# Score products with the keys' low parts: from zero-padded operands on 128 rows of the array to 64 rows, one row half for each half of the keys

## The chip, the core and the metric

The kernel runs on one core of a Trainium2 chip. The metric is the time of one execution on the device in microseconds, as the median of several runs. The engines are named as in the profile: PE is the tensor engine (its matmuls), PEld its weight loads, DVE the vector engine, ACT the scalar engine, POOL GpSimd, and SP the engine that issues most of the DMAs.

## The reference

One layer over 1024 positions of width 1024. The input is normalised and modulated, projected, mixed by 16 attention heads of width 64 in two groups, gated, projected back, added to the input and normalised again. Eight heads (FoX) use a softmax with a forget bias, eight (stick-breaking) a product of sigmoids:

```python
def _fox_block(q, k, v, f_q, f_k, q_pos, k_pos):
    s = jnp.einsum('bhqd,bhkd->bhqk', q, k).astype(jnp.float32) * scale
    s = s + (f_q[..., :, None] - f_k[..., None, :])
    p = jax.nn.softmax(jnp.where(causal, s, -jnp.inf), axis=-1)
    return jnp.einsum('bhqk,bhkd->bhqd', p.astype(v.dtype), v)

def _stick_breaking_block(q, k, v, q_pos, k_pos):
    z = jnp.einsum('bhqd,bhkd->bhqk', q, k).astype(jnp.float32) * scale
    log_keep = jnp.where(strict, jax.nn.log_sigmoid(-z), 0.0)
    later = lax.cumsum(log_keep, axis=3, reverse=True) - log_keep
    w = jnp.where(strict, jnp.exp(jax.nn.log_sigmoid(z) + later), 0.0)
    return jnp.einsum('bhqk,bhkd->bhqd', w.astype(v.dtype), v)

h = u @ w_in[layer]                # queries, keys, values, gates of both groups
# per block of 128 queries: the two functions above, over the keys up to the block's end
y = concat(y_fox * silu(fg), y_sb * silu(sg)) @ w_out[layer]
x = layer_norm(alpha * x + gate * y)
```

Both groups begin with the scores q times k over a head's 64 components. These score products are what the change is about.

## The kernel before

All operands are float32. To keep precision at the fast rate, the kernel splits an operand into a high part, rounded to the type float32r, and a low part, the rest, and forms three of the four products: high x high, low x high and high x low. The projections do so with three matmuls per step (L255 to L257).

For the scores, the head's 64 components fill only half of the array's 128 rows, so two of the three products share one matmul. For each pair of heads p and each head h in it, the query tile `qst[p][h]` holds the scaled queries' high part on the head's own 64 partitions (`r` in the code) and their low part on the other 64 (`o`); the key tile `kst[p][h]` holds the keys' high part on both halves (ScalarE writes one, a DMA copies it to the other, L240 to L242). One matmul over 128 rows (L410) thus gives high x high plus low x high.

The third product, the queries' high part times the keys' low part, is a second matmul into the same place (L411). The keys' low parts of both heads of a pair lie in one tile, `klo[p]`: head 0 on partitions 0 to 63, head 1 on 64 to 127 (L243). As stationary operand it takes a tile `z` of 128 partitions out of `qz`: the head's own 64 partitions hold the block's queries, copied by ScalarE for every block (`att_query`, L388), and the other 64 hold zeros, set once at the start by GpSimd (L100 to L102), so that the other head's low parts count for nothing.

The work is cut into units (p, h, i): 8 pairs, 2 heads, 8 blocks of 128 queries, 128 units in all. Unit i needs the keys up to `ke = (i + 1) * 128`. Its scores go to the tile `S`, two PSUM banks of 512 columns, of which there is one for the whole kernel. Up to 512 keys fill one bank; more are cut into two equal parts, one in each bank (`ns`, `w`). Pairs 0 to 3 are stick-breaking heads: ScalarE reads `S` twice (L430, L431). Pairs 4 to 7 are FoX heads: VectorE reads it once (L417). Later, lagging two units, PE transposes the weights (L461) and multiplies them with the values (`att_pv`, L476); there the low parts' products use 64 columns of the array.

The order on PE is written out by hand: in a loop over the units, each unit's score products are followed by a measured number of steps of the remaining matmul work (projections of later pairs, the output projection, called fillers), the transposes of an earlier unit, and value products. The query copy of the next unit is issued right behind a unit's scores. The other engines' order is set by a scheduler that also places the waits.

Of the kernel before, what the change touches and what calls it, by code (L numbers as in the profile page):

```python
# [8 lines left out]
F32 = mybir.dt.float32  # L9
F32R = mybir.dt.float32r  # L10
AF = mybir.ActivationFunctionType
ALU = mybir.AluOpType

P = 128
# [4 lines left out]
HD = 64  # L19
# [8 lines left out]
def tile_hybrid_layer(  # L28
# [17 lines left out]
    nc = tc.nc  # L46
# [9 lines left out]
    def att_tile(name, dt=F32):  # L56
        return big("att", 6, name, dt)
# [13 lines left out]
    def s_tile(name):  # L71
        return ps.tile([P, 2, 512], F32, tag="S", bufs=1, name=name)
# [8 lines left out]
    def after(*instructions):  # L81
        stack = ExitStack()
        for i in instructions:
            stack.enter_context(tc.issue_after(i.ins))
        return stack
# [11 lines left out]
    nc.gpsimd.memset(half.bitcast(F32), 0.5)  # L97

    qz = [[cp.tile([P, P], F32R, tag=f"qz{h}{b}", name=f"qz{h}{b}") for b in range(2)] for h in range(2)]
    for h in range(2):  # L100
        for t in qz[h]:
            nc.gpsimd.memset(t.bitcast(F32), 0.0)  # L102
    gate = cp.tile([P, D], F32, tag="gate", name="gate")
    mhalf = cp.tile([P, 1], F32, tag="mhalf", name="mhalf")
    nc.gpsimd.memset(mhalf, -0.5)
# [55 lines left out]
    for kt in range(NB):  # L161
        nc.tensor.matmul(sc_all[:, kt // 4, kt % 4 * P:][:, :P], sc[:, kt:kt + 1].to_broadcast([P, P]), ident,
                         start=True, stop=True)
# [71 lines left out]
    def evac_k(p, ch, acc, kst, klo, heads):  # L235
        s = slice(ch * 512, ch * 512 + 512)
        for h in heads:
            r = slice(h * HD, h * HD + HD)
            o = slice((1 - h) * HD, (1 - h) * HD + HD)
            first = nc.scalar.copy(kst[h][r, s], acc[r, :])  # L240
            kf = kst[h].bitcast(F32)
            nc.sync.dma_start(kf[o, s], kf[r, s])  # L242
            last = nc.vector.tensor_tensor(klo[r, s], acc[r, :], kf[r, s], op=ALU.subtract)  # L243
        return first, last

    def evac_g(p, ch, acc, sg):
# [12 lines left out]
    qst, kst, klo, sgt, vt = {}, {}, {}, {}, {}  # L259
# [11 lines left out]
    def evac_m(p, m, ch, acc, heads=(0, 1)):  # L271
        if m == 0:
            evac_q(p, ch, acc, qst[p], heads)
        elif m == 1:
            return evac_k(p, ch, acc, kst[p], klo[p], heads)
        else:
            evac_g(p, ch, acc, sgt[p])
# [102 lines left out]
    zq = {}  # L380
    turn = [0, 0]

    def att_query(u):
        p, h, i = u
        zq[u] = z = qz[h][turn[h] % 2]
        turn[h] += 1
        r = slice(h * HD, h * HD + HD)
        nc.scalar.copy(z[r, :], qst[p][h].bitcast(F32)[r, i * P:i * P + P])  # L388

    def att_causal(u):  # L390
        p, h, i = u
        if p >= 4:
            f = fb[2 * (p - 4) + h]
            dg = slice(i * P, i * P + P)
            nc.vector.tensor_tensor(f[:, dg], f[:, dg], ps_causal[0][:, :P] if ps_causal else causal, op=ALU.add)

    def att_scores(u, following):
        p, h, i = u
        z = zq.pop(u)
        ke = (i + 1) * P  # L400
        ns = 1 if ke <= 512 else 2
        w = ke // ns
        qs = slice(i * P, i * P + P)
        dg = slice(ke - P, ke)
        if p >= 4:
            f = fb[2 * (p - 4) + h]
        S = s_tile(f"S_{p}_{h}_{i}")
        for s in range(ns):
            ks = slice(s * w, s * w + w)
            nc.tensor.matmul(S[:, s, :w], qst[p][h][:, qs], kst[p][h][:, ks], start=True, stop=False)  # L410
            nc.tensor.matmul(S[:, s, :w], z, klo[p][:, ks], start=False, stop=True)  # L411
        v3 = lambda a: a[:, :ke].rearrange("p (a b) -> p a b", a=ns)
        if p >= 4:
            a = att_tile(f"a_{p}_{h}_{i}")
            nm = sb.tile([P, 1], F32, tag="nm", bufs=4, name=f"nm_{p}_{h}_{i}")
            l = sb.tile([P, 1], F32, tag="l", bufs=4, name=f"l_{p}_{h}_{i}")
            rows = nc.vector.tensor_tensor_reduce(out=v3(a), in0=S[:, :ns, :w], in1=v3(f),  # L417
                                           op0=ALU.add, op1=ALU.min, scale=-1.0, scalar=BIG,
                                           accum_out=nm)
            if following:  # L420
                with after(rows):
                    att_causal(following)
            nc.scalar.activation(a[:, :ke], a[:, :ke], AF.Exp, scale=-1.0, bias=nm, accum_out=l)  # L423
            nc.vector.reciprocal(l, l)  # L424
            nc.gpsimd.tensor_scalar(a[:, :ke], a[:, :ke], l, 1.0, op0=ALU.mult, op1=ALU.mult)  # L425
            st_w[u] = a
        else:
            kp = att_tile(f"kp_{p}_{h}_{i}")
            be = att_tile(f"be_{p}_{h}_{i}")
            nc.scalar.activation(v3(kp), S[:, :ns, :w], AF.Sigmoid, scale=-1.0)  # L430
            nc.scalar.activation(v3(be), S[:, :ns, :w], AF.Sigmoid)  # L431


            n = min(ke, 512)
            rv = kp[:, ke - n:ke][:, ::-1]
            scan = nc.vector.tensor_tensor_scan(rv, rv, floor[0][:, 512 - n:][:, ::-1], initial=0.0,  # L436
                                                op0=ALU.mult, op1=ALU.max)
            if ke > n:
                rv = kp[:, :ke - n][:, ::-1]
                scan = nc.vector.tensor_tensor_scan(rv, rv, floor[0][:, 0:1].to_broadcast([P, ke - n]),  # L440
                                                    initial=kp[:, ke - n:ke - n + 1], op0=ALU.mult, op1=ALU.max)
            with after(scan):
                att_causal(following)
            nc.gpsimd.tensor_tensor(be[:, :ke - 1], be[:, :ke - 1], kp[:, 1:ke], op=ALU.mult)  # L444
            nc.gpsimd.memset(be[:, ke - 1:ke], 0.0)
            st_w[u] = be
# [195 lines left out]
    for kb in range(NB):  # L642
        last = kb == NB - 1
# [95 lines left out]
    for kb in range(NB):  # L739
# [13 lines left out]
        if kb < len(evacs):  # L753
            n, h = evacs[kb]
# [196 lines left out]
    for k in range(len(units) + LAG + 1):  # L951
        if k < len(units):
            if k == 16 * 4 - 1:
                load_fb(0)
                load_fb(1)
            if k == 0:
                att_query(units[0])
            with after(*last_evac if k == 0 else ()):
                att_scores(units[k], units[k + 1] if k + 1 < len(units) else None)
            if k == 16 * 4 - 1:  # L960
                ps_causal.append(ps.tile([P, 512], F32, tag="fl", bufs=1, name="ps_causal"))
                nc.scalar.copy(ps_causal[0][:, :P], causal)
            if k + 1 < len(units):
                att_query(units[k + 1])
            p, h, i = units[k]
            if 4 <= p < NPAIR - 1 and i == 0:
                load_fb(2 * (p - 4) + h + 2)
# [3 lines left out]
        if LAG <= k < len(units) + LAG:  # L971
            u = units[k - LAG]
# [78 lines left out]
```

## Time and profile before

| | |
|---|---|
| median of 3 runs | 691.55 us (691.04 to 691.66) |
| the profiled execution | 691.02 us, of which its span 689.3 us |
| granted clock of PE, mean | 0.996 |
| score products L410, L411 | 192 matmuls each |
| copies of queries into `qz`, L388 | 128 |

A row of the timeline gives start and duration in microseconds, the engine, the line, the operation, what is written from what, and the shape. Of a matmul, `128*128` is the number of array rows times array columns that it uses, and `128x384` the size of the output. Matmuls are pipelined, so that their recorded durations overlap: the distance from one start to the next tells what a matmul takes from the engine. In a row of grouped instructions, the number behind the bar is the busy time in microseconds, then the mean in nanoseconds, then the idle time in front of these instructions.

### The profile page before, as it was taken

To read this page: it belongs to the slowest core of one execution; us is meant where nothing else is said; L and a number is where in the kernel's file an instruction comes from. 1 tells how busy PE (TensorE), PEld (TensorE's weight loads), DVE (VectorE), ACT (ScalarE), POOL (GpSimd) and SP (SyncE) were. 2 spreads that over 40 slices of the span, in tenths; PEclk is the share of its full clock that TensorE was granted. 3 is DMA by queue.
4 is the path that set the end of the run, shared out by engine and by line. 5 is a ranking of instruction groups with operands and counts; after the bars stand their busy time and mean duration, and the time that the engine had idled before them with its cause. 6 is when DMAs were issued, how large, how long until landed. Compare 5 with 4: busy or idle time off the path is not lost. (4 is left out here: it accounts for less than half of the span.)

```text
span 689.3 us, 11785 instructions
## 1 busy us (share of the span) xinstructions
PE 673.6 (98%) x4033; PEld 589.7 (86%) x4033; DVE 453.9 (66%) x923; ACT 379.8 (55%) x858; POOL 430.4 (62%) x556
## 2 busy tenths in 40 slices
PE   8999999999999999999999999999999999999995
PEld 5789898888998888889998888899988889888884
DVE  5985458767656676676675665665566667774644
ACT  5666457856567666575665564655565667521000
POOL 4567977656438565556398897867584364655422
PEclk9999999999999999999999999999999999999998
DMA  8956241011102122112134555353251298153301
GB/s 314 416 225 241 72 121 45 25 40 53 39 9 70 41 55 55 38 49 60 38 137 139 185 166 160 101 165 127 100 150 39 80 310 320 58 175 104 120 31 61
DMA packets 44028, 81.59 MB, mean 118 GB/s; under 512 B 5120, under 2 KB 18880, under 8 KB 43072
## 3 DMA queue, kind: packets, MB, share of 16 engines
q1 hardware_dynamic: 42816, 76.65, 33.8%
q10 hardware_dynamic: 1152, 4.19, 2.0%
q8 instruction: 32, 0.52, 0.3%
q14 instruction: 28, 0.23, 0.1%
HBM read 60.34 MB, written 16.29 MB: 111 GB/s over the span
## 5 line engine op out<-in xcount | busy, mean ns | idle before, releaser
L255 PE MATMUL m<-uh,whi 128*128 128x512 f32 x304 | 126.3, 416 | 0.5 <-DVE kl L243 0.5
L256 PE MATMUL m<-ul,whi 128*128 128x512 f32 x304 | 119.8, 394 | 0.0
L257 PE MATMUL m<-uh,wlo 128*128 128x512 f32 x304 | 119.6, 394 | 0.0
L464 DVE TENSOR_TENSOR pt<-T,pt 128x512 fp32r<-128x512 f32 (+2 forms) x192 | 100.5, 550 | 17.9 <-ACT pt L463 16.8
L444 POOL TENSOR_TENSOR be<-be,kp 128x127 f32<-128x127 f32 (+3 forms) x64 | 77.1, 1205 | 34.5 <-DVE kp L440 24.7
L463 ACT CAST pt<-T 128x512 fp32r<-128x512 f32 (+2 forms) x192 | 85.7, 480 | 16.8 <-PE T L461 13.0
L436 DVE TENSOR_TENSOR_SCAN kp<-kp,floor 128x512 f32<-128x512 f32 (+2 forms) x64 | 65.2, 1018 | 32.1 <-ACT kp L430 31.3
L476 PEld LDWEIGHTS pv<-pt,v 128*128 128x128 f32 (+1 forms) x640 | 77.2, 163 | 4.5 <-DVE pt L464 0.7
L476 PE MATMUL pv<-pt,v 128*128 128x256 f32 (+3 forms) x640 | 80.5, 271 | 0.5 <-DVE pt L464 0.5
L425 POOL TENSOR_SCALAR a<-a,l 128x1024 f32<-128x1024 f32 (+3 forms) x64 | 47.9, 748 | 43.3 <-DVE l L424 29.8
L257 PEld LDWEIGHTS m<-uh,wlo 128*128 128x128 f32 x304 | 57.1, 188 | 13.5
L423 ACT ACTIVATE a<-a,nm 128x1024 f32<-128x1024 f32 (+3 forms) x64 | 49.8, 778 | 34.1 <-DVE nm L417 33.0
L410 PE MATMUL S<-k,q 128*128 128x512 f32 (+5 forms) x192 | 66.5, 348 | 0.2 <-DVE nm L417 0.2
L411 PE MATMUL S<-kl,qz 128*128 128x512 f32 (+5 forms) x192 | 65.5, 342 | 0.0
L255 PEld LDWEIGHTS m<-uh,whi 128*128 128x128 f32 x304 | 57.3, 188 | 9.2 <-DVE kl L243 0.9
L256 PEld LDWEIGHTS m<-ul,whi 128*128 128x128 f32 x304 | 57.4, 189 | 7.9
L497 POOL TENSOR_TENSOR ty<-ty,sg 64x256 f32<-64x256 f32 x64 | 47.4, 741 | 25.4 <-DVE ty L496 12.8
L417 DVE CUSTOM_DVE_ANT_0 a<-S,fb 128x1024 f32<-128x1024 f32 (+3 forms) x64 | 48.3, 755 | 20.4 <-PE S L411 9.3
L430 ACT ACTIVATE kp<-S 128x128 f32<-128x128 f32 (+3 forms) x64 | 41.7, 651 | 31.8 <-PE S L411 28.3
L310 PE MATMUL v<-whi_v,uh 128*128 128x256 f32 (+1 forms) x192 | 56.0, 292 | 0.7 <-DVE kl L243 0.7
L388 ACT CAST qz<-q 64x128 fp32r<-64x128 f32 x128 | 37.4, 295 | 33.0 <-PE S L411 31.9
L312 PE MATMUL v<-wlo_v,uh 128*128 128x256 f32 (+1 forms) x192 | 54.2, 282 | 0.0
(287 smaller groups left out, 1612.9 us busy)
## 6 DMA issues: line engine op xcount, KB each, us to landing
raw<-in_w_qkg_dram SPq DMA_DIRECT2D x38, 256.0 KB, 2.9
wss<-in_w_ss_dram SPq DMA_DIRECT2D x7, 1024.0 KB, 9.1
x<-in_x_dram SPq DMA_DIRECT2D x8, 512.0 KB, 7.0
k<-k SPq DMA_DIRECT2D x32, 128.0 KB, 2.4
wg<-in_w_gate_dram SPq DMA_DIRECT2D x8, 512.0 KB, 4.4
raw_o<-in_w_out_dram SPq DMA_DIRECT2D x16, 256.0 KB, 2.7
fb<-f_dr ACTq DMA_DIRECT2D x8, 512.0 KB, 4.2
wo_dr<-whi_o SPq DMA_DIRECT2D x16, 256.0 KB, 2.4
```

Of the source, the lines that this page charges most:

```text
L255: nc.tensor.matmul(acc, hi[:, c], u_hi[kt][:, s], start=(kt == 0), stop=False)
L256: nc.tensor.matmul(acc, hi[:, c], u_lo[kt][:, s], start=False, stop=False)
L257: nc.tensor.matmul(acc, lo[:, c], u_hi[kt][:, s], start=False, stop=(kt == NB - 1))
L310: nc.tensor.matmul(acc[:, :n], u_hi[kt][:, ts_], hi[:, s], start=(kt == 0), stop=False)
L312: nc.tensor.matmul(acc[:, :n], u_hi[kt][:, ts_], lo[:, s], start=False, stop=(kt == NB - 1))
L410: nc.tensor.matmul(S[:, s, :w], qst[p][h][:, qs], kst[p][h][:, ks], start=True, stop=False)
L411: nc.tensor.matmul(S[:, s, :w], z, klo[p][:, ks], start=False, stop=True)
L436: scan = nc.vector.tensor_tensor_scan(rv, rv, floor[0][:, 512 - n:][:, ::-1], initial=0.0, op0=ALU.mult, op1=ALU.max)
L444: nc.gpsimd.tensor_tensor(be[:, :ke - 1], be[:, :ke - 1], kp[:, 1:ke], op=ALU.mult)
L463: nc.scalar.copy(hi[:, :n, qo:qo + P], t3)
L464: nc.vector.tensor_tensor(lo[:, :n, qo:qo + P], t3, hi.bitcast(F32)[:, :n, qo:qo + P], op=ALU.subtract)
L476: nc.tensor.matmul(acc[:m, q0:256], vt[p][:, kb, h * P:h * P + m], pt[:, kb % 4, q0:], start=start, stop=stop)
```

## The change

The third product now uses 64 rows of the array, without the zeros. For the first 512 keys, the keys' low parts lie on the head's own partitions as before, and the stationary operand is `qst` itself, its 64 partitions with the high part. For the keys from 512 on, the low parts are written to the other 64 partitions (`evac_k`, where `ch` is the half of the keys), and the stationary operand is the tile `z`, into which ScalarE copies the queries on those other partitions. That copy is made only for units with i of 4 or more. The two heads of a pair still share the tile `klo[p]`: where one head has its first half, the other has its second.

A unit with more than 512 keys is now cut at 512: the first bank holds 512 columns, the second the rest. The order of its four products is: high parts for the second bank, high parts for the first bank, low parts for the first bank, low parts for the second bank. The two low products of such a unit use different rows of the array and different banks. The zeroing of `qz` is gone. The readers of `S` take it as one row of `ke` columns.

```diff
     qz = [[cp.tile([P, P], F32R, tag=f"qz{h}{b}", name=f"qz{h}{b}") for b in range(2)] for h in range(2)]
-    for h in range(2):
-        for t in qz[h]:
-            nc.gpsimd.memset(t.bitcast(F32), 0.0)
...
-            last = nc.vector.tensor_tensor(klo[r, s], acc[r, :], kf[r, s], op=ALU.subtract)
+            last = nc.vector.tensor_tensor(klo[o if ch else r, s], acc[r, :], kf[r, s], op=ALU.subtract)
...
     def att_query(u):
         p, h, i = u
+        if i < 4:
+            return
         zq[u] = z = qz[h][turn[h] % 2]
         turn[h] += 1
         r = slice(h * HD, h * HD + HD)
-        nc.scalar.copy(z[r, :], qst[p][h].bitcast(F32)[r, i * P:i * P + P])
+        o = slice((1 - h) * HD, (1 - h) * HD + HD)
+        nc.scalar.copy(z[o, :], qst[p][h].bitcast(F32)[r, i * P:i * P + P])
...
-        ns = 1 if ke <= 512 else 2
-        w = ke // ns
...
-        for s in range(ns):
-            ks = slice(s * w, s * w + w)
-            nc.tensor.matmul(S[:, s, :w], qst[p][h][:, qs], kst[p][h][:, ks], start=True, stop=False)
-            nc.tensor.matmul(S[:, s, :w], z, klo[p][:, ks], start=False, stop=True)
-        v3 = lambda a: a[:, :ke].rearrange("p (a b) -> p a b", a=ns)
+        r = slice(h * HD, h * HD + HD)
+        o = slice((1 - h) * HD, (1 - h) * HD + HD)
+        banks = [(0, min(ke, 512))] + ([(512, ke)] if ke > 512 else [])
+        for b, (k0, k1) in reversed(list(enumerate(banks))):
+            nc.tensor.matmul(S[:, b, :k1 - k0], qst[p][h][:, qs], kst[p][h][:, k0:k1], start=True, stop=False)
+        for b, (k0, k1) in enumerate(banks):
+            w, rows = (zq.pop(u), o) if b else (qst[p][h][:, qs], r)
+            nc.tensor.matmul(S[:, b, :k1 - k0], w[rows, :], klo[p][rows, k0:k1], start=False, stop=True)
+        S = S.rearrange("p a b -> p (a b)")[:, :ke]
...
-            nc.scalar.activation(v3(kp), S[:, :ns, :w], AF.Sigmoid, scale=-1.0)
-            nc.scalar.activation(v3(be), S[:, :ns, :w], AF.Sigmoid)
+            nc.scalar.activation(kp[:, :ke], S, AF.Sigmoid, scale=-1.0)
+            nc.scalar.activation(be[:, :ke], S, AF.Sigmoid)
```

How the order on PE changes is seen at a unit with 768 keys, head 1, block i = 5 of the first pair. In the names, `S` is the score tile, `k`, `q` and `kl` are the tiles `kst`, `qst` and `klo`; the last column is the size of the output. Before:

```order
L461 MATMUL T_1_2_0_1466<-ident,be_1_2_1368 128x128 x3
L410 MATMUL S_1_5_1472<-k_1_249,q_1_247 128x384
L411 MATMUL S_1_5_1472<-kl_250,qz_83 128x384
L410 MATMUL S_1_5_1472<-k_1_249,q_1_247 128x384
L411 MATMUL S_1_5_1472<-kl_250,qz_83 128x384
L255 MATMUL m_2_1_1427<-uh_116,whi_2_1_1243 128x512
```

And after the change:

```order
L463 MATMUL T_1_2_0_1454<-ident,be_1_2_1357 128x128 x3
L408 MATMUL S_1_5_1460<-k_1_245,q_1_243 128x256
L408 MATMUL S_1_5_1460<-k_1_245,q_1_243 128x512
L413 MATMUL S_1_5_1460<-kl_246,q_1_243 128x512
L413 MATMUL S_1_5_1460<-kl_246,qz_83 128x256
L252 MATMUL m_2_1_1415<-uh_112,whi_2_1_1235 128x512
```

Both high products now stand first, the shorter ahead, and the two low products follow one another; the neighbours on both sides are of the same kind as before. The number of matmuls of the unit stays four.

On ScalarE, the place is around the units with i = 1 and 2 of the same head, where the copies into `qz` stand between the readings of the scores. Before:

```order
L430 ACTIVATE kp_1_1_1336<-S_1_1_1333 128x256
L431 ACTIVATE be_1_1_1337<-S_1_1_1333 128x256
L388 CAST qz_83<-q_1_247 64x128
L463 CAST pt_0_0_3_0_1310<-T_0_7_0_1344 128x4x128
L463 CAST pt_0_0_3_1_1319<-T_0_7_1_1351 128x4x128
L430 ACTIVATE kp_1_2_1367<-S_1_2_1364 128x384
L431 ACTIVATE be_1_2_1368<-S_1_2_1364 128x384
L388 CAST qz_82<-q_1_247 64x128
```

And after the change:

```order
L432 ACTIVATE kp_1_1_1326<-S_1_1_1323 128x256
L433 ACTIVATE be_1_1_1327<-S_1_1_1323 128x256
L465 CAST pt_0_0_3_0_1300<-T_0_7_0_1333 128x4x128
L465 CAST pt_0_0_3_1_1309<-T_0_7_1_1340 128x4x128
L432 ACTIVATE kp_1_2_1356<-S_1_2_1353 128x384
L433 ACTIVATE be_1_2_1357<-S_1_2_1353 128x384
```

The copies for the blocks with i below 4 are gone, and what stood around them keeps its order.

More of the change, by code (lines that the diff above doesn't have):

```diff
@@ L398, in att_scores @@
         p, h, i = u
-        z = zq.pop(u)
         ke = (i + 1) * P
-        ns = 1 if ke <= 512 else 2
-        w = ke // ns
         qs = slice(i * P, i * P + P)
-        dg = slice(ke - P, ke)
         if p >= 4:
@@ L416, in att_scores @@
             l = sb.tile([P, 1], F32, tag="l", bufs=4, name=f"l_{p}_{h}_{i}")
-            rows = nc.vector.tensor_tensor_reduce(out=v3(a), in0=S[:, :ns, :w], in1=v3(f),
+            rows = nc.vector.tensor_tensor_reduce(out=a[:, :ke], in0=S, in1=f[:, :ke],
                                            op0=ALU.add, op1=ALU.min, scale=-1.0, scalar=BIG,
```

## The prediction

> **What bounds the kernel now.** I read the page's busy shares first, then the list of who waited for whom on the tensor engine, then its busy time over the stretch in which the score products run.
>
> ```profile
> PE 673.6 (98%) x4033; PEld 589.7 (86%) x4033; DVE 453.9 (66%) x923; ACT 379.8 (55%) x858; POOL 430.4 (62%) x556
> ```
> ```profile
> PE sc_all L162 <- DVE sc L159: 3.2, 1, 3.2
> PE T L461 <- DVE pt L464: 0.9, 2, 0.8
> ...
> PE S L410 <- DVE nm L417: 0.2, 1, 0.2
> ```
> ```profile
> 91.00:616.00 525.00, 522.04 (x3297) 467.02 (x3296) 356.04 (x748) 324.67 (x764) 340.73 (x433) 1.00 0.32 100
> ```
>
> The second fence gives microseconds in all, times, longest; in the third the columns after the stretch and its length are the busy time of PE, PEld, DVE, ACT and POOL, then the granted clock. Between 91 and 616 us PE is busy for 522.04 of 525 us at the full clock, and the one score product that waited did so once, for 0.2 us. Nobody feeds PE too late: in this stretch a nanosecond that PE loses or saves is one of the whole. So only the time from one matmul's start to the next one's matters, and that is read from the timeline, because the recorded durations overlap:
>
> ```profile
> 300.69 0.39 PE L255 MATMUL m<-uh,whi 128*128 128x512 f32 x1
> 300.92 0.39 PE L256 MATMUL m<-ul,whi 128*128 128x512 f32 x1
> 301.15 0.40 PE L257 MATMUL m<-uh,wlo 128*128 128x512 f32 x1
> 301.38 0.34 PE L410 MATMUL S<-k,q 128*128 128x384 f32 x1
> 301.56 0.34 PE L411 MATMUL S<-kl,qz 128*128 128x384 f32 x1
> 301.73 0.34 PE L410 MATMUL S<-k,q 128*128 128x384 f32 x1
> 301.91 0.34 PE L411 MATMUL S<-kl,qz 128*128 128x384 f32 x1
> 302.08 0.39 PE L255 MATMUL m<-uh,whi 128*128 128x512 f32 x1
> 302.31 0.39 PE L256 MATMUL m<-ul,whi 128*128 128x512 f32 x1
> ```
>
> Start and duration stand first. From 300.69 to 302.31, eight matmuls stream 4 x 512 + 4 x 384 = 3584 columns in 1.62 us: 0.452 ns a column, whatever the line, each starting while the one before is still recorded.
>
> **The change part by part.** *Columns saved.* Each of the 128 units (8 pairs, 2 heads, 8 query blocks) multiplies its keys' low parts once. Before, all ke = 128(i+1) columns go through one after the other. Now, for i = 4 to 7, the ke - 512 columns of the second bank can pass beside the first 512, on the array's other 64 rows. Those are 128 + 256 + 384 + 512 = 1280 columns a head, 20480 over 16 heads, x 0.452 ns = **-9.3 us** if the two products run at the same time. The 64 units with i < 4 save nothing.
>
> *The new split of the high products* (512 and the rest, instead of two equal parts) keeps the number of columns and of instructions. Its shortest product, 128 columns ahead of a long one, has a row:
>
> ```profile
> 247.47 0.40 PE L257 MATMUL m<-uh,wlo 128*128 128x512 f32 x1
> 247.71 0.22 PE L410 MATMUL S<-k,q 128*128 128x128 f32 x1
> 247.77 0.28 PE L411 MATMUL S<-kl,qz 128*128 128x128 f32 x1
> 247.88 0.45 PE L255 MATMUL m<-uh,whi 128*128 128x512 f32 x1
> ```
> ```profile
> 247.71 0.19 PEld L411 LDWEIGHTS S<-kl,qz 128*128 128x128 f32 x1
> 247.82 0.19 PEld L255 LDWEIGHTS m<-uh,whi 128*128 128x128 f32 x1
> ```
>
> The product behind a 128-column one starts 0.06 us later, at 128 x 0.452 ns; only behind two short ones in a row does the weights' load (0.11 from 247.71 to 247.82) set the pace. Here one short one stands ahead of a long one: **0**.
>
> *The change of the array's form.* The low products now use 64 of the 128 rows; everything around them uses 128. That is two changes of form per unit, 256 in all, and no instruction of the trace before uses 64 rows. So the price c of one change is bounded by rows. Below: nothing. The nearest rows are the value products, nearly half of which use 64 of the columns (128*64):
>
> ```profile
> 206.49 0.29 PE L312 MATMUL v<-wlo_v,uh 128*128 128x264 f32 x1
> 206.61 1.00 PE L476 MATMUL pv<-pt,v 128*128 128x256 f32 x8
> 207.45 0.71 PE L461 MATMUL T<-ident,be 128*128 128x128 f32 x5
> ```
> ```profile
> L476 PE MATMUL pv<-pt,v 128*128 128x256 f32 x272 | 53.7, 286 | 0.0
> L476 PE MATMUL pv<-pt,v 128*64 128x256 f32 x240 | 39.2, 281 | 0.5 <-DVE pt L464 0.5
> ```
>
> The group of eight holds six products of 256 columns and two of 128, 1792 columns, and goes to 64 columns and back; it takes 207.45 - 206.61 = 0.84 us against 0.81 for its columns. A change of columns thus costs 0.02 us at most. But all 128 rows stay in use there, so the weights of one form can be loaded behind the other as always. Above: a change that lets nothing overlap. A matmul that could not have its weights loaded ahead stands at 176.63, where PE had waited:
>
> ```profile
> 176.63 0.19 PEld L310 LDWEIGHTS v<-whi_v,uh 128*128 128x128 f32 x1 [0.88 <-DVE kl L243]
> 176.63 0.39 PE L310 MATMUL v<-whi_v,uh 128*128 128x264 f32 x1 [0.74 <-DVE kl L243]
> ...
> 176.86 0.28 PE L311 MATMUL v<-whi_v,ul 128*128 128x264 f32 x1
> ...
> 176.99 0.28 PE L312 MATMUL v<-wlo_v,uh 128*128 128x264 f32 x1
> 177.11 0.28 PE L310 MATMUL v<-whi_v,uh 128*128 128x264 f32 x1
> ```
>
> It takes 0.39 us instead of 0.28, and the next starts 0.23 instead of 0.12 later: 0.11 us for the exposed load. Waiting in addition until the old matmul is through adds the recorded tail, 0.28 - 0.12 = 0.16, so 0.27 us at most. If the new load merely starts when the old columns have all entered and the matmul follows at the distance of 247.82 to 247.88, it is 0.06.
>
> I take c = 0.11 us, the exposed load: a load for half the rows stands between weights in use and weights waiting for all rows, in neither of which it fits as a whole, so I expect that it isn't pulled ahead, and nor is the full load after it. 256 x 0.11 = **+28.2 us** (bounds 0 and 69.1). With loads exposed, the second bank's load also comes 0.11 behind the first's. For i = 7 (512 beside 512) that lengthens the pair by 0.11; for i = 6 by 384 x 0.452 ns + 0.11 - 0.23 = 0.05; below that it is covered: 16 x 0.16 = **+2.6 us** (0 if nothing is exposed).
>
> The Trainium skill's "TensorEngine Tiling (Array Packing)", Tiling Modes, Key Properties, speaks against the change: altering the tiling mode, not merely the tile, drains the TensorE. It gives no price. By it c would lie above zero and the time anywhere above 682, up to the upper bound below; without it, at 682. The value products' 0.02 us does not agree with a drain at every change of tile size, but "PSUM — Partial Sum Buffer", The four PSUM rules, remarks that float32r matmuls force the whole column group, so that these products may never leave the full mode; no run here shows which holds.
>
> *Casts and memsets taken away.*
>
> ```profile
> L388 ACT CAST qz<-q 64x128 fp32r<-64x128 f32 x128 | 37.4, 295 | 33.0 <-PE S L411 31.9
> ```
> ```profile
> L102 POOL MEMSET qz<- x4: 204/204/205, 1.7 to 2.2; 128x128 f32 x4
> ```
>
> 64 of 128 casts go, 64 x 295 ns = 18.9 us of ScalarE, and 0.8 us of GpSimd before the first 3 us are over. ScalarE is at 55%, and PE's list of waits has no row for the cast; **0**. The other 64 casts have more time than now, because the product that reads one is the last of its unit's four, where it was the second. The subtraction that makes the keys' low parts writes to other partitions for half of the keys but has the same size: **0**. Were ScalarE's slack gone, half the casts would be worth at most those 18.9 us. No wait is added; the readers of the scores wait, as now, for the last product of a unit, and what comes late is only what PE itself delays: the next fillers.
>
> *Sum.* 691.0 (the profiled execution; its span is 689.3, with 1.7 around it) - 9.3 + 28.2 + 2.6 = 712.5; the runs' median is 0.5 higher, so **713 us**. With c = 0.06 and no second delay it is 691.5 - 9.3 + 15.4 = 698; with 0.27 it is 691.5 - 9.3 + 69.1 + 2.6 = 754. The forecast's own range is 698 to 754.
>
> **The rivals.** *No price, two products at once* (the other side). At the score products, the low loads for both halves are pulled ahead under the 512-column high product (0.23 us, room for two loads at a pace of 0.11), and both stream together: 691.5 - 9.3 = **682 us**. For it speaks that the value products change form for nothing and that PE is the bound, so no other engine takes the gain back. Against it, no row shows loads for parts of the rows. It decides as long as c stays under 9.3 / 256 = 0.036 us. "TensorE: Matmul & The Clock Gate" in the Trainium skill, Part 3, Measured speedup, has four 32-row tiles with 512 columns at 3.07 times the speed; by it the two products would overlap as this rival needs, and no run here shows it yet. It says nothing of going in and out of such tiles.
>
> *No price, but one after the other* (the change doesn't do what it says). The order on the engine keeps the low products as two instructions; if the second only starts when the first has streamed, all columns are there as before, at 0.452 ns: **691.5 us**. For it speaks that in the timeline above every matmul starts only when the one before has streamed its columns; against it, that these two share neither rows nor a bank.
>
> **How the numbers follow.** Forecast 0.53, no price at once 0.36, one after the other 0.11. The time is the forecast's, 713. The range has to reach to 682 on one side, less 1 for waits that shrink, so 681; above, of the forecast's own range the part over 740 (c over 0.22 us, where hardly anything would overlap) holds perhaps 0.12, and is left out. A change under 0.2%, 1.4 us, can't be told from none here: faster is the first rival, 0.36; the same is the second with a little of c near 0.036 us, less what falls outside, 0.10; slower 0.54.
>
> **What would show it.** In the changed kernel's timeline, at a unit with i < 4: the low product, marked 64*128, should start 0.11 us or more beyond its predecessor's columns, and the filler behind it likewise; if both starts keep the 0.452 ns a column, c is nothing. At i = 7 the two low products should start about 0.11 us apart; if 0.23 apart, they run one after the other. PE's count of matmuls stays 4033 and its waits stay small; if instead long waits of PE for other engines appear, the reasoning from PE alone was wrong. The casts' row should read x64. The forecast is wrong if the time is under 693.

## The result

The changed kernel takes 728.15 us (727.92 to 728.22), the kernel before 691.47 us in the runs beside it: a ratio of 1.0531, 95% interval [1.0518, 1.0544], or 36.7 us slower. The profiled execution of the changed kernel has a span of 726.4 us against 689.3. The forecast was slower, 713 us, in a range from 681 to 740; of the slower cases that it bounded (698 to 754), the time came out above the middle.

The page's busy shares of the changed kernel:

```profile
PE 710.8 (98%) x4033; PEld 575.7 (79%) x4033; DVE 454.9 (63%) x923; ACT 363.5 (50%) x794; POOL 429.6 (59%) x552
```

PE is still busy for 98% and runs as many matmuls. The weight loads are busy for 575.7 us instead of 589.7, which is 79% of a longer span; most of the difference is that the two loads of a pair now lie on top of each other (64 x 0.18 = 11.5 us, see the rows below). ScalarE lost 64 instructions and 16 us, and the span did not follow. PE's own waits for other engines, in the list of who waited for whom (us in all, times, longest), are as small as before:

```profile
PE sc_all L159 <- DVE sc L156: 3.0, 1, 3.0
PE xT_early L209 <- ACT x L195: 0.9, 2, 0.5
...
PE T L463 <- DVE pt L466: 0.7, 1, 0.7
```

So the 37 us lie in the matmuls' own sequence. Here is the timeline at a unit with i = 6 (896 keys), PE first, then the weight loads of the same stretch:

```profile
172.32 0.56 PE L408 MATMUL S<-k,q 128*128 128x384 f32 x2
172.82 0.50 PE L413 MATMUL S<-kl,q 64*128 64x512 f32 x1
172.82 0.44 PE L413 MATMUL S<-kl,qz 64*128 64x384 f32 x1
173.25 0.50 PE L252 MATMUL m<-uh,whi 128*128 128x512 f32 x1
173.58 0.39 PE L253 MATMUL m<-ul,whi 128*128 128x512 f32 x1
173.81 0.39 PE L254 MATMUL m<-uh,wlo 128*128 128x512 f32 x1
```
```profile
172.81 0.18 PEld L413 LDWEIGHTS S<-kl,q 64*128 64x128 f32 x1 [0.30 <-issue]
172.82 0.18 PEld L413 LDWEIGHTS S<-kl,qz 64*128 64x128 f32 x1
173.24 0.19 PEld L252 LDWEIGHTS m<-uh,whi 128*128 128x128 f32 x1 [0.24 <-issue]
173.35 0.19 PEld L253 LDWEIGHTS m<-ul,whi 128*128 128x128 f32 x1
173.58 0.19 PEld L254 LDWEIGHTS m<-uh,wlo 128*128 128x128 f32 x1
```

Three things stand in these rows. The two low products do start together, at 172.82 (in all 64 pairs at most 4 ns apart). The load for the first of them begins at 172.81, only when the matmul begins, while in 128-row form a load runs one matmul ahead (173.58 for L254 at 173.81); the matmul is therefore recorded with 0.50 us instead of 0.39. And the load of L252 behind them is exposed in the same way, at 173.24: again 0.50 instead of 0.39, and L253 follows after 0.33 instead of 0.23.

A unit with i = 2, 384 keys, where there is nothing to pair, shows the price by itself:

```profile
192.47 0.28 PE L309 MATMUL v<-wlo_v,uh 128*128 128x264 f32 x1
192.59 0.34 PE L408 MATMUL S<-k,q 128*128 128x384 f32 x1
192.86 0.44 PE L413 MATMUL S<-kl,q 64*128 64x384 f32 x1
193.23 0.39 PE L307 MATMUL v<-whi_v,uh 128*128 128x264 f32 x1
193.46 0.29 PE L308 MATMUL v<-whi_v,ul 128*128 128x264 f32 x1
```

384 columns are 0.174 us. The low product starts 0.27 after the high one, 0.09 too late; the next matmul 0.37 after that, 0.20 too late; and the one behind it 0.23 after, instead of 0.12, 0.11 too late. Over all 128 units the medians from the records are 0.094, 0.196 and, before fillers and value products, 0.107 us: **0.397 us for going into the 64-row form and coming out**. We read it as a hold of 0.09 each way, in which the matmul waits beyond its predecessor's columns, and a weight load of 0.105 each way that nothing covers; the sixth experiment separates the two.

Adding up starts, the stretches from a unit's first score product to the next other matmul grew from 72.0 to 98.3 us, the matmul just behind them lost 12.0, and all else on PE got 0.8 shorter. From the first matmul's start to the last one's that is 37.4 us, which is the result.

### The profile page after: what moved, and what is told of

Its sections match the earlier page's. It is cut to its first block, busy times and chain, and to the rows that moved or that the text cites. A ratio compares the mean times of both kernels' runs of the same rounds, so it can differ in the third digit from the quotient of the medians.

```text
span 726.4 us, 11732 instructions
## 1 busy us (share of the span) xinstructions
PE 710.8 (98%) x4033; PEld 575.7 (79%) x4033; DVE 454.9 (63%) x923; ACT 363.5 (50%) x794; POOL 429.6 (59%) x552
## 4 chain that ended last, share of the span: by engine, by line
PE 92%; DMA 3%; DVE 2%; POOL 1%; issue 1%; SPq 0%; ACT 0%; POOLq 0%; DVEq 0%
PE m L252 12%; PE pv L478 10%; PE m L253 10%; PE m L254 9%; PE T L463 9%; PE S L413 6%; PE v L307 5%; PE S L408 5%; PE o L839 4%; PE o L837 4%; PE o L838 4%; PE v L309 4%; PE v L308 4%; DMA wss<-in_w_ss_dram 3%; PE st_late L571 1%
## 5 line engine op out<-in xcount | busy, mean ns | idle before, releaser
L252 PE MATMUL m<-uh,whi 128*128 128x512 f32 x304 | 133.7, 440 | 0.4 <-DVE kl L240 0.4
L253 PE MATMUL m<-ul,whi 128*128 128x512 f32 x304 | 119.8, 394 | 0.0
L254 PE MATMUL m<-uh,wlo 128*128 128x512 f32 x304 | 119.6, 394 | 0.0
L252 PEld LDWEIGHTS m<-uh,whi 128*128 128x128 f32 x304 | 57.2, 188 | 22.9 <-issue 13.6
L254 PEld LDWEIGHTS m<-uh,wlo 128*128 128x128 f32 x304 | 57.1, 188 | 13.7
L253 PEld LDWEIGHTS m<-ul,whi 128*128 128x128 f32 x304 | 57.5, 189 | 7.0
L307 PE MATMUL v<-whi_v,uh 128*128 128x256 f32 (+1 forms) x192 | 58.4, 304 | 0.4 <-DVE kl L240 0.4
L413 PE MATMUL S<-kl,q 64*128 64x512 f32 (+3 forms) x128 | 57.9, 452 | 0.0
L408 PE MATMUL S<-k,q 128*128 128x128 f32 (+3 forms) x192 | 57.0, 351 | 0.0
L498 DVE TENSOR_TENSOR ty<-pv,ty 64x256 f32<-64x256 f32 x64 | 26.9, 420 | 46.2 <-ACT ty L497 34.1
L497 ACT COPY ty<-pv 64x256 f32<-64x256 f32 x64 | 23.4, 366 | 64.6 <-PE pv L478 50.8
```

The lines of the kernel that those rows point to most:

```text
L252: nc.tensor.matmul(acc, hi[:, c], u_hi[kt][:, s], start=(kt == 0), stop=False)
L253: nc.tensor.matmul(acc, hi[:, c], u_lo[kt][:, s], start=False, stop=False)
L254: nc.tensor.matmul(acc, lo[:, c], u_hi[kt][:, s], start=False, stop=(kt == NB - 1))
L307: nc.tensor.matmul(acc[:, :n], u_hi[kt][:, ts_], hi[:, s], start=(kt == 0), stop=False)
L408: nc.tensor.matmul(S[:, b, :k1 - k0], qst[p][h][:, qs], kst[p][h][:, k0:k1], start=True, stop=False)
L413: nc.tensor.matmul(S[:, b, :k1 - k0], w[rows, :], klo[p][rows, k0:k1], start=False, stop=True)
```

## The experiments

The theory after the result: each change between 128 and 64 rows costs a hold and an open weight load, together 0.186 us as the mean from the records above ((26.3 + 12.0 + 9.3) / 256, with the 9.3 us that the pairs save); inside the form everything runs as well as before, and pairs run at once. The rivals put the price into the pairs, the new split, the unit rather than the change, or each 64-row product.

**Half of the changes undone.** Units with i < 4 use zeros and 128 rows again:

```diff
...
-        if i < 4:
-            return
-        zq[u] = z = qz[h][turn[h] % 2]
-        turn[h] += 1
+        zq[u] = z = (qp if i < 4 else qz)[h]
...
-        nc.scalar.copy(z[o, :], qst[p][h].bitcast(F32)[r, i * P:i * P + P])
+        nc.scalar.copy(z[r if i < 4 else o, :], qst[p][h].bitcast(F32)[r, i * P:i * P + P])
...
+            if i < 4:
+                w, rows = zq.pop(u), slice(0, P)
+            else:
+                w, rows = (zq.pop(u), o) if b else (qst[p][h][:, qs], r)
```

> The 64 units with i < 4 go back to the zero-padded operand on 128 rows (one buffer per head for it instead of two); the units with i of 4 and more keep the 64-row pairs. Theory (each change between 128 and 64 rows costs 0.186 us, as the starts in the changed kernel's trace add up: 0.09 hold and 0.1 for a weight load that stands open): 128 changes fewer, 728.2 - 128 x 0.186 = 704 us. Rival (the price lies in the pairs, with their two row halves, two banks and uneven split): near 728 us.

Measured: 706.64 us, ratio 1.0219 [1.0204, 1.0235]. 128 changes fewer took 21.5 us away, 0.168 each, 2.3 us less than by the mean. Up to 1.7 of these come from the 16 units with 128 keys, which paid for weight loads already in the kernel before (see the seventh experiment): with 128 keys, two products of 0.058 us each run at the pace of their loads, 0.11. The rest is not traced. The price does not lie in the pairs alone: the 64 units that gave up the form had none. The 64 units that kept their pairs are 15.2 us above the kernel before although they save 9.3, so a change costs (15.2 + 9.3) / 128 = 0.19 there too.

**The split and the order alone.** The kernel before, with 512 and the rest:

```diff
-        for s in range(ns):
-            ks = slice(s * w, s * w + w)
-            nc.tensor.matmul(S[:, s, :w], qst[p][h][:, qs], kst[p][h][:, ks], start=True, stop=False)
-            nc.tensor.matmul(S[:, s, :w], z, klo[p][:, ks], start=False, stop=True)
...
+        banks = [(0, min(ke, 512))] + ([(512, ke)] if ke > 512 else [])
+        for b, (k0, k1) in reversed(list(enumerate(banks))):
+            nc.tensor.matmul(S[:, b, :k1 - k0], qst[p][h][:, qs], kst[p][h][:, k0:k1], start=True, stop=False)
+        for b, (k0, k1) in enumerate(banks):
+            nc.tensor.matmul(S[:, b, :k1 - k0], z, klo[p][:, k0:k1], start=False, stop=True)
```

> The kernel before with only the new split (512 and the rest) and the new order (both high products first); the low products on 128 rows with zeros. Theory: no change of form, so 691.5 us, within 1. Rival (the uneven split or the order of the four products costs part of the 36.7 us): 695 us or more.

Measured: 693.16 us, ratio 1.0026 [1.0016, 1.0035], 1.7 us slower, beyond the 1 us that the expectation allowed. The rival's 695 us is not reached, so the split and the order are not what costs 36.7 us; but the split is not free. It shows at units with i = 4, in this kernel's timeline:

```profile
264.30 0.39 PE L257 MATMUL m<-uh,wlo 128*128 128x512 f32 x1
264.53 0.51 PE L408 MATMUL S<-k,q 128*128 128x128 f32 x2
264.87 0.46 PE L410 MATMUL S<-kl,qz 128*128 128x512 f32 x2
265.16 0.45 PE L255 MATMUL m<-uh,whi 128*128 128x512 f32 x1
265.45 0.39 PE L256 MATMUL m<-ul,whi 128*128 128x512 f32 x1
```

The 128 and 512 columns of the two high products are 0.29 us, but take 0.34 (264.53 to 264.87); L255, behind the low product of 128 columns, takes 0.29 instead of 0.23. Each 128-column product hides only half of a load, and the matmul behind it pays the other 0.054: 32 such products x 0.054 = 1.7 us. In the changed kernel itself only the 16 high ones count, an estimated 0.9 us, since the low ones run beside 512 columns; its records show the low products of these 16 units 0.047 us later than those of the others.

**The pairing taken away.** Both halves of the low parts stay on the head's own rows, so that the two products follow each other:

```diff
...
-            last = nc.vector.tensor_tensor(klo[o if ch else r, s], acc[r, :], kf[r, s], op=ALU.subtract)
+            last = nc.vector.tensor_tensor(klo[r, s], acc[r, :], kf[r, s], op=ALU.subtract)
...
     def att_query(u):
         p, h, i = u
-        if i < 4:
-            return
+        return
...
-            w, rows = (zq.pop(u), o) if b else (qst[p][h][:, qs], r)
-            nc.tensor.matmul(S[:, b, :k1 - k0], w[rows, :], klo[p][rows, k0:k1], start=False, stop=True)
+            nc.tensor.matmul(S[:, b, :k1 - k0], qst[p][h][r, qs], klo[p][r, k0:k1], start=False, stop=True)
```

> The changed kernel, but the low parts of both halves of the keys stay on the head's own 64 rows, so that the two low products can't run at once; no copies of queries at all. Theory: 20480 columns more, 0.452 ns each: 728.2 + 9.3 = 737.5 us, same number of changes of form. Rival (the pairs save nothing beyond what the records show, since they start together but share the array): 728 us.

Measured: 737.33 us, ratio 1.0662 [1.0645, 1.068]; 9.2 us above the changed kernel. The pairs save what their columns are worth. All of ScalarE's copies of queries are gone here and bring nothing.

**Twice the changes in a unit.**

```diff
-        for b, (k0, k1) in enumerate(banks):
             w, rows = (zq.pop(u), o) if b else (qst[p][h][:, qs], r)
             nc.tensor.matmul(S[:, b, :k1 - k0], w[rows, :], klo[p][rows, k0:k1], start=False, stop=True)
```

The last two lines moved into the loop over the high products, so that each high product is followed by its low one.

> The changed kernel with the order high, low for the second bank, then high, low for the first: units with i of 4 and more change form four times instead of twice and lose the pairing. Theory: 128 more changes x 0.186 = 23.8 and 9.3 for the columns: 761 us. Rival (a price per unit that uses 64 rows, not per change): 737 us.

Measured: 761.51 us, ratio 1.1013 [1.0997, 1.1029]. The price is paid per change: without the 9.3 us for the lost pairing, 128 changes added 24.1 us, 0.188 each.

**Longer stays in the form.** Each unit's low products stand in a loop that runs three times (`for t in range(3):`, with `stop=t == 2`).

> The changed kernel with each unit's low products issued three times over (so the low term counts three times in the scores). Theory: inside the 64-row form loads are ahead of their matmuls as in the 128-row form, so only columns are added: 106496 x 0.452 ns = 48.1, 776 us. Rival (every 64-row product shows its weight load, 0.1 us more for each of the 256 repetitions): 803 us.

Measured: 776.66 us, ratio 1.1232 [1.1215, 1.1248]: 48.5 us more, against 48.1 for the columns alone. The rival's 803 us is far off. In its timeline, a unit with i = 2 shows the price at both ends and nothing between; matmuls, then loads:

```profile
126.60 0.34 PE L408 MATMUL S<-k,q 128*128 128x384 f32 x1
126.86 0.79 PE L415 MATMUL S<-kl,q 64*128 64x384 f32 x3
127.58 0.86 PE L480 MATMUL pv<-pt,v 128*128 128x256 f32 x5
```
```profile
126.86 0.47 PEld L415 LDWEIGHTS S<-kl,q 64*128 64x128 f32 x3 [0.30 <-issue]
127.58 0.77 PEld L480 LDWEIGHTS pv<-pt,v 128*128 128x128 f32 x6 [0.25 <-issue]
```

Three products of 384 columns are 0.52 us; from 126.86 to 127.58 it is 0.72, the same 0.20 too much as behind a single one. Their loads are busy for 0.47 us in all, hardly longer than the open load and the first two products take (0.105 + 0.35): from the second on they are ahead again. Products of 128 columns are too short to hide a load, as the last experiment shows.

**A smaller weight load.** The low products are formed for 64 queries of each block, so that their weights have 64 columns:

```diff
-            nc.tensor.matmul(S[:, b, :k1 - k0], qst[p][h][:, qs], kst[p][h][:, k0:k1], start=True, stop=False)
+            nc.tensor.matmul(S[:, b, :k1 - k0], qst[p][h][:, qs], kst[p][h][:, k0:k1], start=True, stop=True)
...
-            nc.tensor.matmul(S[:, b, :k1 - k0], w[rows, :], klo[p][rows, k0:k1], start=False, stop=True)
+            nc.tensor.matmul(S[:HD, b, :k1 - k0], w[rows, :HD], klo[p][rows, k0:k1], start=False, stop=True, skip_group_check=True)
```

> The changed kernel, but the low products are formed for the first 64 queries of each block only (the low term is left out for the others), so that their weights have 64 columns instead of 128. Theory (about half of the price on the way in is a weight load that stands open, in proportion to its columns; in the kernel before, loads of 64 columns took 135 ns against 188): 128 x 0.053 = 6.8 us less, 721 us. Rival (the price is a fixed hold, not a load): 728 us.

Measured: 721.79 us, ratio 1.0439 [1.0421, 1.0456], 6.4 us below the changed kernel, 0.050 for each of 128 ways in. A unit with i = 2:

```profile
230.39 0.34 PE L408 MATMUL S<-k,q 128*128 128x384 f32 x1
230.66 0.38 PE L413 MATMUL S<-kl,q 64*64 64x384 f32 x1
230.97 0.50 PE L252 MATMUL m<-uh,whi 128*128 128x512 f32 x1
231.31 0.39 PE L253 MATMUL m<-ul,whi 128*128 128x512 f32 x1
```

The recorded low product shrank from 0.44 to 0.38 and the next one starts after 0.31 instead of 0.37. The start of the low product itself has not moved, 0.27 after the high one. So the part of about 0.105 is a load that scales with its columns, and the hold of 0.09, which stays, is something else.

**Short products kept apart**, an attempt at a faster kernel from the kernel before. In units with 128 keys, one filler step goes between the two short products (pairs 0 to 6):

```diff
+            if i == 0 and p < NPAIR - 1:
+                fill(done[0] + 1)
             nc.tensor.matmul(S[:, s, :w], z, klo[p][:, ks], start=False, stop=True)
```

> The kernel before, but in units with i = 0 (128 keys) of pairs 0 to 6 one step of filler matmuls is put between the two 128-column products, so that no two short products follow one another. Theory (a weight load of 0.11 us paces matmuls of 128 columns, 0.058 us, only where two short ones follow): 14 units x 0.1 = 1.4 to 1.5 us less, 690.0 us. Rival (scores that are ready a step later hold up what reads them): 691.5 us or more.

Measured: 695.68 us, ratio 1.0055 [1.0042, 1.0069]; slower, and the theory behind it was wrong. Its timeline at such a unit:

```profile
219.75 0.40 PE L257 MATMUL m<-uh,wlo 128*128 128x512 f32 x1
219.99 0.22 PE L410 MATMUL S<-k,q 128*128 128x128 f32 x1
220.05 0.45 PE L255 MATMUL m<-uh,whi 128*128 128x512 f32 x1
220.33 0.39 PE L256 MATMUL m<-ul,whi 128*128 128x512 f32 x1
```

A lone short product between long ones is paid for as well: L255 takes 0.28 us instead of 0.23. A 128-column product costs its 0.054, together or apart, so there was nothing to gain. As for the loss, PE's list of waits now has two rows that the kernel before has not, and one that has grown from 0.9:

```profile
PE gate L717 <- POOL be L447: 2.3, 1, 2.3
PE T L463 <- DVE pt L466: 1.9, 3, 1.0
...
PE S L410 <- ACT be L433: 0.5, 1, 0.5
```

These add 3.8 us, of the 6.0 by which this execution (697.61 us) lies behind the kernel before. That the moved fillers bring these waits about is likely but was not tested, and the rest is not traced.

**Where the form would pay.** Six times each low product, in the kernel before and in the changed one.

> The kernel before with each low product issued six times (the low term counts six times in the scores). Only columns are added: 5 x 73728 x 0.452 ns = 166.6, and 0.05 us for each of 80 short repetitions at the pace of their loads: 858 to 862 us.

> The changed kernel with each low product issued six times. Theory (the price is paid per change of form and not per product, and pairs run at once): 728.2 + 5 x 24.2 = 849 us, which is 9 to 13 us less than the kernel before with six of them. Rival (repeated pairs don't gain): 858 us or more.

Measured: 859.71 us (ratio 1.2431 [1.2408, 1.2453]) and 853.12 us (1.2335 [1.2313, 1.2358]). With six times the work inside the form, the kernel with the changes of form is 6.6 us faster instead of 36.7 slower. A repetition costs 33.6 us in the kernel before and 25.0 in the changed one; the expectation for the latter was too low, since its repeated products of 128 columns run at the pace of their loads too, which had been counted only on the other side. A unit with 128 keys of the changed kernel with six shows it:

```profile
159.62 0.22 PE L408 MATMUL S<-k,q 128*128 128x128 f32 x1
159.77 0.88 PE L415 MATMUL S<-kl,q 64*128 64x128 f32 x6
160.58 0.50 PE L252 MATMUL m<-uh,whi 128*128 128x512 f32 x1
```

From 159.77 to 160.58 it is 0.81 us, of which 6 x 0.058 = 0.35 are columns and 0.20 the usual excess; the other 0.26 are five repetitions that take 0.11 each instead of 0.058. Over 16 units that makes some 4 us, by which 849 was too low.

No version here beats the kernel before.

## Why the prediction was right in direction and short in size

*What bounds the kernel.* Right. PE's sequence sets the time: its starts add up to 37.4 us, beside the result's 36.7.

*Columns saved, -9.3 us.* Right: 9.2 us between the kernels with and without the pairing.

*The new split, 0.* Wrong by an estimated 0.9 us in the changed kernel (1.7 when alone). The quoted rows show the start behind a short product on time and the one after that 0.05 late (247.77 to 247.88). The prediction put this down to two short products in a row; the second and the seventh experiment show that one is enough.

*The change of form, c = 0.11 us, +28.2.* This is the term that failed in size. It expected that a load for half the rows isn't pulled ahead, nor the full load after it; that is right, with 0.105 measured where 0.11 was taken. The reason that it gave, that such a load fits neither the weights in use nor those waiting, no run tests. What is missing is the hold of 0.09 each way, which the prediction had listed as part of its upper bound ("waiting in addition until the old matmul is through", 0.16) and left out of its value. With the time 36.7 = 256 c + 0.9 - 9.3, c is 0.176 on average. The units' own rows give 0.397 / 2 = 0.199; of the difference of 5.7 us, 1.7 is what the 16 shortest units paid before anyway, 0.8 that transposes behind 15 units lose only 0.055, and some 3 us are unassigned (of these, 0.8 is what the rest of PE got shorter by, and 0.7 lies between the starts' 37.4 and the result's 36.7).

The row of the trace before that was weighed against a price, the value products at 64 columns, says nothing about rows. The Trainium skill's "TensorEngine Tiling (Array Packing)", Tiling Modes, Key Properties, has the TensorE drained when the tiling mode changes. The hold of 0.09 us at a change of rows agrees with this, though no run shows that it is such a drain; the load that is exposed for 0.105 comes on top. For 64 columns the trace shows no hold (the 0.02 us at most of the prediction).

*The second load behind the first, +2.6.* Wrong: in all 64 pairs the two loads start 3 or 4 ns apart, as do the two matmuls. The loads for the two row halves run at once.

*Casts and memsets, 0.* Right, the third experiment took all copies away and only the columns showed.

*The sum.* 713 against 728.15: 256 x 0.066 = 16.9 too little for c, 0.9 missing for the split, 2.6 too much for the second load; together 15.2. That this closes is no proof, since the 0.176 was worked out from the result; the figures apart from it are the 0.168 per change of the first experiment and the 0.188 of the fourth.

*The rivals.* "No price, two products at once" was right in its second half and wrong in the first. "One after the other" fell with the starts at 172.82 and with the third experiment.

Still open is what the hold of 0.09 us is: it does not depend on the load's size, and it appears in front of the low product as well as behind it. No experiment took it apart further.

## What to carry to other kernels

A product on 64 rows between products on 128 rows costs about 0.4 us here for the way in and out, as much as 880 columns; two half-row products side by side save at most 512 columns of it. Where PE sets the time, use the form only where several pairs can stand together, as in the run with six, and otherwise fill the other rows with zeros: the kernel before paid for those with engines that had time. As an estimate from the two prices of a repetition, 33.6 and 25.0 us, the 36.7 us are made up after 36.7 / 8.6 = 4.3 repetitions beyond the first; half of the units here have no pair. When bounding an unknown price, add the parts of a bound that can occur together before choosing the middle.

## What was not expected of the hardware

Loads for the two row halves run at the same time (starts 3 ns apart in the median, 4 at most), although loads of the 128-row form follow one another at 0.11 us (247.71 to 247.82). Inside the 64-row form loads are ahead again from the second product on, for the products of 384 columns shown. And a single product of 128 columns (0.058 us) makes the matmul after the next one start 0.054 us late, in the two places shown, at 264.53 and at 219.99.
